# Entry into the attention stage: tile-wise pool waits, an earlier scale, an earlier table, a later first split

## The chip, the cores and the metric

The kernel runs as one program on one core of a Trainium2 chip. The metric is the device time of one execution in microseconds. Three executions of the kernel before took 1218.88, 1219.09 and 1220.08 us; the median, 1219.09 us, is the time before.

## What is computed

One layer of an encoder block on x of 1024 tokens by 1024 channels:

```python
u = rms_norm(x, g1)
q, k, v, cB, cC, cH, gA, gB = split(u @ w_in)        # 512 x 6, then 1024 x 2
q, k = rms_norm per head (8 heads of 64)
yA = neighbourhood_attention(q, k, v, rpb) @ w_attn_branch
yB = (cB * conv3(cC * cH)) @ w_conv_branch            # depthwise, width 3
x  = x + (sigmoid(gA) * yA + sigmoid(gB) * yB) @ w_o
x  = x + relu(rms_norm(x, g2) @ w_mlp_in)**2 @ w_mlp_out
```

The tokens form a grid of 16 rows by 64 columns. Each query sees a window of 8 rows by 16 columns, clamped inside the grid, with a learned bias.

## The kernel before

**Numbers.** Every operand of a product is held as two 16-bit floats, a high and a low part, and a product is three passes (high by high, high by low, low by high). A weight arrives as 32-bit "raw" pieces. Its chunk is scaled by a power of two and split: ScalarE writes the high part (L310), VectorE the low part (L301, `raw * scale - high`).

**How a chunk is prepared.** `Chunk.prep` is a Python generator that emits a few instructions at each resumption. For a conv chunk (kind C, four pieces of 128 x 768) it emits, in order:

1. four squares with a running sum on ScalarE (L263), one in each resumption;
2. the sum of the four and its product on VectorE (L267, L269), which writes one bf16 column of `ones`; then it waits until `units` has gone up by three;
3. the matmul by a matrix of ones that adds the column over the partitions (L201), on TensorE, into a bank of kind "d";
4. six resumptions on VectorE that turn the sum into a power of two and its products with the row gains (L204, L425, L427, L429, L431 with L432, L279);
5. the split, one piece in a resumption: ScalarE's high part of piece p beside VectorE's low part of piece p-1, and the load of a later raw piece on SyncE's queue.

`tick(n)` resumes the front generator of the list `bg` n times. While `forced[0]` is set, the waits on `units` inside the generators are passed over.

**The order around the change.** Everything is emitted in one program order for each engine, under a manual schedule; an engine takes its instructions strictly in that order. K's eight token blocks are finished by `qk_vec` (L612 to L632: ScalarE and VectorE in turn) and turned by a DMA transpose into `kD` (`finish_qk`, L643). After the last K products TensorE does two units of 24 matmuls for the first conv chunk into two banks of kind "o". Then the attention loop starts: 64 steps, and some more to empty the pipeline. Step k emits:

- the scores of step k into a bank of kind "s" (`at_qk`, L831), of which there are three, so step k waits until the maximum of step k-3 has been read;
- 7 or 8 conv matmuls (`emit`, L911);
- the bias and the maximum of step k-1 on VectorE (`at_max`, L845), which writes a tile `sz`;
- the exponential of step k-1 on ScalarE (`at_exp`, L854), the reciprocal of a pair of sums (L858, L859), the high part of the probabilities (L867, four steps behind) and the low part (L871, five behind);
- one step of the conv work (`conv_post`, `conv_taps`): ScalarE's copies of the two first banks into `z` (L719), the product with `z` (L724), the taps (L740, L744, and L747 and L750 on GpSimd);
- up to three resumptions of the background generator (`fill`), as long as `room()` holds. Two numbers in `debt` say how many ns of work VectorE and ScalarE have been given beyond 2150 ns a step, `spend` adds to them, and `room()` asks that both lie under 2350;
- from step 11 on, at odd steps, the product of the probabilities with V (`at_pv`, L888).

**Pools.** A pool may lie where closed pools lay. K's working tiles (`gq`, `qs`, `sq`, `q16`, `s16`) lie in `pqk`, closed just ahead of the attention loop; the loop's own tiles (`sz`, `z`, `cv`, `P16`, `PT`) lie in `p2`. In the kernel before, the pools `pbias`, `p2`, `wab`, `p3` and `p4` are opened without the argument `reuse_waits`, whose default is "pool": what first uses the new pool on an engine waits for everything that used the closed pools beneath it. With "tile", a tile waits for those old tiles alone whose bytes it takes over. In the layout of the program before, `z` lies over the last bytes of tiles of an earlier stage, over `gq` and over the start of one `s16`; the five `sz` lie over `s16`; the `q16` tiles, which the K transposes read, lie under `cv` alone. Pool `p5`, at the end, already has "tile".

**ScalarE's tables.** The exponential needs another activation table than the square root. The last square root of the K stage (L412) is in block 15 of `qk_vec`; the first exponential is that of attention step 0.

Of the kernel before, what the change touches and what calls it, by code (L numbers as in the profile page):

```python
# [14 lines left out]
AF = mybir.ActivationFunctionType  # L15
# [37 lines left out]
def encoder_block(ctx: ExitStack, tc: tile.TileContext, x, weights, cols, gqk, rel, masks, out):  # L53
    nc = tc.nc
    V, A, G, T, SP = nc.vector, nc.scalar, nc.gpsimd, nc.tensor, nc.sync
# [10 lines left out]
    def bank(tag):  # L66
        return psum.tile([128, 512], F32, name="ps_" + tag, tag=tag, bufs=banks[tag])
# [11 lines left out]
    sc = base.tile([128, 512], F32, name="sc")  # L79
# [3 lines left out]
    def cols_of(kind, n):  # L83
        a = area[kind]
        if a[1] + n > a[2]:
            assert kind != "keep"
            a[1] = a[0]
        a[1] += n
        return slice(a[1] - n, a[1])

    def keep(n=1):
        return cols_of("keep", n)

    def tmp(n=1):
        return cols_of("tmp", n)
# [25 lines left out]
    def advance(g):  # L121
        try:
            return next(g) or True
        except StopIteration:
            return False

    def step(n=1):
        for _ in range(n):
            for g in list(fg):
                if not advance(g):  # L130
                    fg.remove(g)

    def tick(n=1):

        for _ in range(n):
            i = 0
            while i < len(bg):
                r = advance(bg[i])
                if not r:
                    bg.pop(i)  # L140
                elif r == WAIT and side[0]:
                    i += 1
                else:
                    break
# [3 lines left out]
    def spend(v=0, a=0):  # L148

        debt[0] += v  # L150
        debt[1] += a

    def fill():

        i = 0
        while i < len(bg):
            r = advance(bg[i])
            if not r:
                bg.pop(i)
            elif r != WAIT:  # L160
                return True
            elif not side[0]:
                return False
            else:
                i += 1
        return False

    def drain():
        while fg:
            step()  # L170

    def flush():
        forced[0] = True
        while bg:
            tick()
            step()
        forced[0] = False

    late, units, forced, side = [], [0], [False], [False]
# [27 lines left out]
    def unit(mms, post=None, steps=0, ticks=0):  # L207

        for ps, l, r, a, b in mms:
            T.matmul(ps, l, r, start=a, stop=b)  # L210
        units[0] += 1
        work[0] += len(mms) * mms[0][0].shape[-1]
        settle()
        if post:
            late.append(post)
        for i in range(max(steps, ticks)):
            if i < steps:
                step()
            if i < ticks:
                tick()  # L220

    def settle():
        while late:
            late.pop(0)()


    wpool = {"ws": wsp}
# [109 lines left out]
    def push(*chunks):  # L337
        for ch in chunks:
            bg.append(ch.prep())
# [31 lines left out]
        SP.dma_start(xt[:, b], x[b * 128:(b + 1) * 128, :])  # L371

    gq = wqk.tile([128, 2, HD], F32, name="gq", bufs=1)
    warm = tmp()
    V.memset(sc[:, warm], 1.0)
    A.activation(sc[:, warm], sc[:, warm], AF.Sqrt)
    load_x(0)
# [231 lines left out]
    def qk_vec(ps, inv, kind, res):  # L609
        qs = wqk.tile([128, 512], F32, name="qs", bufs=3)  # L610
        sq = wqk.tile([128, 512], F32, name="sq", bufs=1)
        A.activation(qs, ps, AF.Copy, scale=sc[:, inv])  # L612
        A.activation(sq, qs, AF.Square)
        yield
        ss, y = tmp(8), tmp(8)
        V.tensor_reduce(sc[:, ss], sq.rearrange("p (h d) -> p h d", h=8), axis=AX, op=OP.add)
        yield
        yield from rstd(ss, HD, y, 12 if kind == "q" else 0)
        if kind == "k":
            V.tensor_scalar(sc[:, y], sc[:, y], sc[:, sgq], None, op0=OP.mult)  # L620
            yield
        q3 = qs.rearrange("p (h d) -> p h d", h=8)
        V.tensor_tensor(q3, q3, sc[:, y][:, :, None].to_broadcast([128, 8, HD]), op=OP.mult)
        yield
        if kind == "k":
            V.tensor_tensor(q3, q3, gq[:, 0][:, None, :].to_broadcast([128, 8, HD]), op=OP.mult)
        r = 2 if kind == "q" else 1
        t = wqk.tile([128, 8, 2, r, HD], F16, name=kind + "16", tag="q16")
        q4 = q3[:, :, None, :].to_broadcast([128, 8, r, HD])
        A.activation(t[:, :, 0], q4, AF.Copy)  # L630
        yield
        V.tensor_tensor(t[:, :, 1], q4, t[:, :, 0], op=OP.subtract)  # L632
        res.append(t)
# [4 lines left out]
    def finish_qk(n):  # L638
        kind, b = todo[n]
        while not q16[n]:  # L640
            step()
        dst = QD.rearrange("p a e w t -> p (a e w) t") if kind == "q" else KD
        SP.dma_start_transpose(dst[:, :, b * 128:(b + 1) * 128], q16.pop(n)[0].rearrange("p h w r d -> p (h w r d)"))  # L643

    for n, (kind, b) in enumerate(todo):
        ch = cQ if kind == "q" else cK
        if b == 0:
            push(cK if kind == "q" else cConv[0])
        ps = bank("do"[n % 2])
        q16[n] = []  # L650

        def post(ps=ps, kind=kind, n=n, ch=ch):
            fg.append(qk_vec(ps, ch.inv, kind, q16[n]))
        unit(tok_mms(ps, actU, b, ch, 8, 512, 0), post, 4, 6 if 4 < n < 8 else 3)
        if n == 3:
            forced[0] = True
            while formed[0] < 4:
                step()
            forced[0] = False
            QD = base.tile([128, 4, 2, 2, S], F16, name="qD", tag="Q")  # L660
            KD = base.tile([128, 8, S], F16, name="kD", tag="K")
            pln.close()
            base2 = ctx.enter_context(tc.tile_pool(name="base2", bufs=1))
            BT = base2.tile([128, 2, 4, S], F16, name="bT", tag="B")
            pbias = ExitStack()
            wbias = pbias.enter_context(tc.tile_pool(name="pbias", bufs=2))
            mk = wbias.tile([128, 2, 384], BF16, name="mk", bufs=1)
            SP.dma_start(mk, masks)
            cneg, cinv = keep(), keep()
            V.tensor_scalar(sc[:, cneg], sc[:, isgq], -(2.0 ** -15), None, op0=OP.mult)  # L670
            V.tensor_scalar(sc[:, cinv], sc[:, sgq], 2.0 ** 15, None, op0=OP.mult)
            bias = {0: bias_load(0)}
        if n >= 3:
            finish_qk(n - 3)
        if n in (5, 6):
            bias_make(*bias[0], n - 5)
        if b == 7:
            flush()
# [18 lines left out]
        step()  # L697
    settle()
    finish_qk(15)
    settle()  # L700
    drain()
    pqk.close()
    p2 = ExitStack()
    w2p = p2.enter_context(tc.tile_pool(name="p2", bufs=2))

    def perm(t, half=None):
        v = t.rearrange("p (r b c) -> p b r c", r=16, b=8)
# [97 lines left out]
    def room():  # L805
        return max(debt) < SPAN + 200
# [107 lines left out]
    for k in range(N + 16):  # L914
        p, w = k // 16, k % 16
        if p < 3 and w == 3:
            bias[p + 1] = bias_load(p + 1)
        if p < 3 and w in (12, 14):
            bias_make(*bias[p + 1], (w - 12) // 2)
            spend(550)  # L920
        ok = lambda d: 0 <= k - d < N
        debt[:] = [max(0, v - SPAN) for v in debt]
        spend(1200, 1120)
        if ok(0):
            at_qk(k)
        emit(4)
        if ok(1):
            at_max(k - 1)
        if ok(4):
            at_hi(k - 4)  # L930
        if k % 2 and ok(3):
            at_recip(k - 3)
        if ok(5):
            at_lo(k - 5)
        if k % 2 == 0 and ok(6):
            at_turn(k - 6)
        if ok(1):
            at_exp(k - 1)
        units[0] += 1
        conv_step(1)  # L940
        for _ in range(3):
            if not room() or not fill():
                break
        emit(3 if k < 14 or k % 4 == 0 else 4)
        if k % 2 == 1 and ok(11):
            at_pv(k - 11)
        if ok(14 + k % 2):
            at_out(k - 14 - k % 2, k % 2)
# [14 lines left out]


    p3 = ExitStack()
    wpool["wa"] = wpool["wb"] = p3.enter_context(tc.tile_pool(name="wab", bufs=2))
    w3p = p3.enter_context(tc.tile_pool(name="p3", bufs=2))
    M = (base.tile([128, 8, S], F16, name="mH", tag="K"), base.tile([128, 8, S], F16, name="mL", tag="V"))
    actA = lambda s, k: QD[:, k, 0, s]
    actB = lambda s, k: BT[:, s, k]  # L970
# [230 lines left out]

    p3.close()
    p4 = ExitStack()
    w4p = p4.enter_context(tc.tile_pool(name="p4", bufs=2))
    U2 = (u2T,
          w4p.tile([128, 3, 2, 4, 512], F16, name="u2x", bufs=1))
    HS = [dram.tile([128, 7, 4, 512], F32, name=f"hs{s}") for s in range(4)]
# [606 lines left out]
```

## Time and profile before

| | |
|---|---|
| median of three runs | 1219.09 us (1218.88 to 1220.08) |
| the profiled execution: its own time | 1219.86 us |
| its span, first to last instruction | 1218.0 us |
| TensorE busy | 1194.1 us, 98% |
| VectorE, ScalarE, GpSimd busy | 931.3, 764.4, 423.2 us |
| granted TensorE clock | 1.000 |
| chain that ended last, by engine | TensorE 74%, VectorE 15%, ScalarE 5%, DMA 3% |

The span is divided into the projections V, Q and K (to 147.6 us), the first two conv units (to 158.2), the attention loop beside the rest of the conv work (to 316.7), the gates and branches (to 548.6), the output projection with the second norm (to about 631), and the MLP. In a row of a timeline the first number is the start, the second the length; consecutive rows of one engine overlap by some 0.07 to 0.09 us. PE is TensorE, DVE VectorE, ACT ScalarE, POOL GpSimd; SPq and ACTq are the queues by which SyncE and ScalarE start DMAs. The bracket at the end of a row says how long the engine had been idle and what ended that.

### The profile page before, as it was taken

To read this page: it belongs to the slowest core of one execution; us is meant where nothing else is said; L and a number is where in the kernel's file an instruction comes from. 1 tells how busy PE (TensorE), PEld (TensorE's weight loads), DVE (VectorE), ACT (ScalarE), POOL (GpSimd) and SP (SyncE) were. 2 spreads that over 40 slices of the span, in tenths; PEclk is the share of its full clock that TensorE was granted. 3 is DMA by queue.
4 is the path that set the end of the run, shared out by engine and by line. 5 is a ranking of instruction groups with operands and counts; after the bars stand their busy time and mean duration, and the time that the engine had idled before them with its cause. 6 is when DMAs were issued, how large, how long until landed. Compare 5 with 4: busy or idle time off the path is not lost.

```text
span 1218.0 us, 17069 instructions
## 1 busy us (share of the span) xinstructions
PE 1194.1 (98%) x6294; PEld 572.9 (47%) x6294; DVE 931.3 (76%) x1758; ACT 764.4 (63%) x1186; POOL 423.2 (35%) x276
## 2 busy tenths in 40 slices
PE   5999999999999999999999999999999999999998
PEld 4544444454444444444458444444444444444444
DVE  6667878898468686887877665456448989998997
ACT  6786677777545455436668787687776754646440
POOL 1430003231411111101003465655657472553562
PEclk9999999999999999999999999999999999999999
DMA  7558555756651121226095654355375835335302
GB/s 279 106 186 182 113 124 114 154 111 118 133 143 54 51 69 35 70 62 246 19 184 131 208 190 160 129 187 166 129 284 199 314 127 203 143 134 195 104 35 104
DMA packets 170867, 173.35 MB, mean 142 GB/s; under 512 B 131488, under 2 KB 132000, under 8 KB 166688
## 3 DMA queue, kind: packets, MB, share of 16 engines
q1 hardware_dynamic: 170208, 168.07, 47.6%
q10 hardware_dynamic: 576, 4.19, 0.9%
q8 instruction: 49, 0.80, 0.3%
q14 instruction: 34, 0.28, 0.1%
HBM read 102.51 MB, written 37.75 MB: 115 GB/s over the span
## 4 chain that ended last, share of the span: by engine, by line
PE 74%; DVE 15%; ACT 5%; DMA 3%; issue 2%; SPq 0%; POOL 0%; ACTq 0%; DVEq 0%
PE ps_d L210 26%; PE ps_s L210 23%; PE ps_o L210 16%; PE ps_d L911 7%; DVE w_s L1033 2%; PE ps_s L831 1%; PE ps_o L888 1%; DVE w_ws L301 1%; DMA qD<-q 1%; DVE s L510 1%; DVE u L446 1%; DVE sg L1149 1%; DMA u2T<-v 1%; ACT w_ws L263 1%; DVE w_v L301 1%
## 5 line engine op out<-in xcount | busy, mean ns | idle before, releaser
L210 PEld LDWEIGHTS <-ops 128*128 128x128 f16 x1356 | 132.4, 98 | 157.3
L210 PEld LDWEIGHTS <-w 128*128 128x128 f16 x1368 | 132.8, 98 | 140.5 <-DMA u2T<-v 1.0
L911 PE MATMUL ps_d<-uT,w_ws 128*128 128x512 f16 x528 | 125.0, 379 | 0.0
L210 PE MATMUL ps_d<-ops 128*128 128x512 f16 (+1 forms) x528 | 118.3, 374 | 0.0
L1635 ACT ACTIVATE ops<-hf,sc 128x2048 f16<-128x2048 f32 x26 | 52.0, 2002 | 98.5 <-PE ps_o L210 35.9
L210 PE MATMUL ps_s<-ops 128*128 128x512 f16 x492 | 112.9, 379 | 0.0
L1022 POOL TENSOR_TENSOR tsum<-raw 128x512 f32<-128x512 f32 x28 | 45.8, 1648 | 148.9 <-ACT raw L1008 148.9
L210 PEld LDWEIGHTS <-uT 128*128 128x128 f16 x648 | 63.4, 99 | 68.2 <-issue 5.4
L1215 POOL TENSOR_TENSOR as<-as 128x512 f32<-128x512 f32 x56 | 77.5, 1385 | 40.8 <-ACT as L1495 37.5
L210 PEld LDWEIGHTS <-w_s 128*128 128x128 f16 x588 | 56.8, 98 | 69.5 <-DVE w_s L1033 2.0
L210 PE MATMUL ps_d<-u2x,w 128*128 128x512 f16 (+1 forms) x360 | 80.0, 372 | 0.0
L210 PE MATMUL ps_o<-ops 128*128 128x512 f16 x336 | 77.1, 379 | 0.0
L911 PEld LDWEIGHTS <-w_ws 128*128 128x128 f16 x528 | 51.0, 98 | 52.8
L1637 DVE SCALAR_TENSOR_TENSOR ops<-hf,sc,ops 128x2048 f16<-128x2048 f32 x26 | 72.6, 2791 | 3.5 <-ACT ops L1635 3.5
L1008 ACT ACTIVATE raw<-raw,sc 128x256 f32<-128x256 f32 x172 | 71.1, 496 | 1.9 <-DMA raw<-in_weights 1.9
L210 PE MATMUL ps_o<-u2T,w 128*128 128x512 f16 (+1 forms) x324 | 71.7, 371 | 0.0
L1022 POOL TENSOR_TENSOR gsum<-raw 128x512 f32<-128x512 f32 x14 | 19.0, 1377 | 133.8 <-issue 73.7
L1037 ACT ACTIVATE w<-raw,sc 128x512 f16<-128x512 f32 (+1 forms) x28 | 24.7, 929 | 52.3 <-DVE sc L431 52.3
L210 PE MATMUL ps_s<-u2T,w 128*128 128x512 f16 (+1 forms) x252 | 52.7, 359 | 0.0
L854 ACT ACTIVATE sz<-sz,sc 128x384 f32<-128x384 f32 (+1 forms) x64 | 37.4, 584 | 24.3 <-DVE sc L845 12.5
L1528 DVE TENSOR_TENSOR as<-ps_d,as 128x512 f32<-128x512 f32 (+1 forms) x14 | 9.4, 672 | 55.6 <-ACT as L1547 53.5
L310 ACT ACTIVATE w_ws<-raw,sc 128x512 f16<-128x512 f32 (+2 forms) x72 | 41.0, 638 | 15.6 <-DVE sc L279 15.6
(340 smaller groups left out, 2616.8 us busy)
## 6 DMA issues: line engine op xcount, KB each, us to landing
raw<-in_weights SPq DMA_DIRECT2D x89, 512.0 KB, 5.8
hs<-as SPq DMA_DIRECT2D x16, 1792.0 KB, 8.8
hf<-hs SPq DMA_DIRECT2D x26, 1024.0 KB, 6.7
w2x<-in_weights SPq DMA_DIRECT2D x16, 512.0 KB, 8.3
raw<-in_weights SPq DMA_DIRECT2D x16, 384.0 KB, 3.7
xt<-in_x SPq DMA_DIRECT2D x8, 512.0 KB, 10.1
gs<-s ACTq DMA_DIRECT2D x4, 1024.0 KB, 4.6
x<-in_x SPq DMA_DIRECT2D x8, 512.0 KB, 9.7
```

The source lines that it names most:

```text
L210: T.matmul(ps, l, r, start=a, stop=b)
L301: V.scalar_tensor_tensor(lo, self.raw[p][:, o:o + m], sc[:, c:c + 1], hi, op0=OP.mult, op1=OP.subtract)
L310: A.activation(self.parts[:, 0, f + o:f + o + m], self.raw[p][:, o:o + m], AF.Copy, scale=sc[:, c:c + 1])
L854: A.activation(z, z, AF.Exp, scale=-1.0, bias=sc[:, d["mx"]], accum_out=sc[:, d["sm"]])
L911: T.matmul(ps, l, r, start=a, stop=b)
L1008: A.activation(v, v, AF.Copy, scale=sc[:, at(g, 4 * i + k)])
L1022: G.tensor_tensor(t[:, o], a, b, op=OP.add)
L1033: V.scalar_tensor_tensor(o(1), w, sc[:, s], o(0), op0=OP.mult, op1=OP.subtract)
L1037: A.activation(o(0), w, AF.Copy, scale=sc[:, s])
L1215: sub.tensor_tensor(z[o], z[a], z[b], op=op)
L1635: A.activation(P[:, 1, 0], hf, AF.Copy, scale=sc[:, Rs])
L1637: V.scalar_tensor_tensor(P[:, 1, 1], hf, sc[:, Rs], P[:, 1, 0], op0=OP.mult, op1=OP.subtract)
```

## The change

Six things change, all in emission order or in waits; no arithmetic of the result does.

1. The pools `pbias`, `p2`, `wab`, `p3` and `p4` are opened with `reuse_waits="tile"`.
2. The scalar column `warm`, used at the start to load the square root's table, is kept, and after the last K block an exponential of this one column is emitted.
3. After that, ahead of the attention loop, the generator of the second conv chunk is resumed eight times with `forced` set: the matmul L201, the six VectorE resumptions L204 to L279, and ScalarE's high part of the first piece.
4. Steps 0 and 1 of the loop (the diff's k below 2) resume no background generator.
5. VectorE's fixed charge is 600 instead of 1200 ns in steps 0 to 4.
6. ScalarE's is 500 instead of 1120 ns in steps 0 to 3.

```diff
     gq = wqk.tile([128, 2, HD], F32, name="gq", bufs=1)
-    warm = tmp()
+    warm = keep()
     V.memset(sc[:, warm], 1.0)
     A.activation(sc[:, warm], sc[:, warm], AF.Sqrt)
...
-            wbias = pbias.enter_context(tc.tile_pool(name="pbias", bufs=2))
+            wbias = pbias.enter_context(tc.tile_pool(name="pbias", bufs=2, reuse_waits="tile"))
...
     settle()
     finish_qk(15)
+    A.activation(sc[:, warm], sc[:, warm], AF.Exp)
     settle()
     drain()
+    forced[0] = True
+    tick(8)
+    forced[0] = False
     pqk.close()
     p2 = ExitStack()
-    w2p = p2.enter_context(tc.tile_pool(name="p2", bufs=2))
+    w2p = p2.enter_context(tc.tile_pool(name="p2", bufs=2, reuse_waits="tile"))
...
-        spend(1200, 1120)
+        spend(1200 if k > 4 else 600, 1120 if k > 3 else 500)
...
         for _ in range(3):
-            if not room() or not fill():
+            if k < 2 or not room() or not fill():
                 break
...
-    wpool["wa"] = wpool["wb"] = p3.enter_context(tc.tile_pool(name="wab", bufs=2))
-    w3p = p3.enter_context(tc.tile_pool(name="p3", bufs=2))
+    wpool["wa"] = wpool["wb"] = p3.enter_context(tc.tile_pool(name="wab", bufs=2, reuse_waits="tile"))
+    w3p = p3.enter_context(tc.tile_pool(name="p3", bufs=2, reuse_waits="tile"))
...
-    w4p = p4.enter_context(tc.tile_pool(name="p4", bufs=2))
+    w4p = p4.enter_context(tc.tile_pool(name="p4", bufs=2, reuse_waits="tile"))
```

## Prediction, made before the result was known

> **What bounds the kernel now.** I read the page first, then TensorE's waits, then the timelines of all engines from 150 to 190 us, and last TensorE's few later waits.
>
> ```profile
> span 1218.0 us, 17069 instructions
> PE 1194.1 (98%) x6294; PEld 572.9 (47%) x6294; DVE 931.3 (76%) x1758; ACT 764.4 (63%) x1186; POOL 423.2 (35%) x276
> ...
> PE ps_o L201 <- DVE ones L332: 10.2, 1, 10.2
> ...
> PE ps_s L831 <- DVE sc L845: 2.4, 2, 1.6
> ```
>
> TensorE is the bound, and 24 us of the span are not its work. 10.2 of them are the start, which the change leaves alone. The largest wait after the start is that of the scores L831 for the maxima L845: twice, 2.4 us. The change can win such waits only. TensorE's timeline has them:
>
> ```profile
> 158.17 0.38 PE L831 MATMUL ps_s<-kD,qD 128*128 128x256 f16 x2
> ...
> 159.90 0.38 PE L831 MATMUL ps_s<-kD,qD 128*128 128x256 f16 x2
> ...
> 164.52 0.48 PE L831 MATMUL ps_s<-kD,qD 128*128 128x384 f16 x2 [0.86 <-DVE sc L845]
> ...
> 166.35 0.49 PE L831 MATMUL ps_s<-kD,qD 128*128 128x384 f16 x2
> ...
> 181.70 0.53 PE L888 MATMUL ps_o<-PT,vT 128*64 128x128 f16 x12
> 182.30 0.48 PE L831 MATMUL ps_s<-kD,qD 128*128 128x384 f16 x2
> ...
> 185.85 0.48 PE L831 MATMUL ps_s<-kD,qD 128*128 128x384 f16 x2 [1.55 <-DVE sc L845]
> ...
> 187.78 0.69 PE L888 MATMUL ps_o<-PT,vT 128*64 128x128 f16 x18
> 188.40 0.39 PE L831 MATMUL ps_s<-kD,qD 128*128 128x256 f16 x2
> ```
>
> These are the starts of steps 0, 1, 3, 4, 12, 13 and 14. Steps 0 to 13 take 188.40 - 158.17 = 30.23 us. Unhindered, a step with 256 columns takes 1.73 (159.90 - 158.17) and one with 384 takes 1.83 (166.35 - 164.52). The two products L888 add 0.46 (0.53, less the 0.07 by which the other one, 0.69 long, overlaps the row behind it) and 0.62, the scale's matmul 0.03. That is 2 x 1.73 + 12 x 1.83 + 1.11 = 26.53 us. So the entry loses 3.70 us: the two listed waits and smaller delays between them. After 188.40 the loop runs without one to 316 us. The 3.70 us are what this change is about, 0.30% of the time.
>
> Where they come from stands on the other engines:
>
> ```profile
> 158.56 0.16 DVE L269 TENSOR_TENSOR ones<-sc 128x1 bf16<-128x1 f32 x1
> ...
> 160.02 0.69 DVE L632 TENSOR_TENSOR k<-qs,k 128x512 f16<-128x512 f32 x1 [0.70 <-ACT k L630]
> 160.63 0.33 DVE L799 TENSOR_SCALAR sc<-sc 128x1 f32<-128x1 f32 x4
> 163.97 0.48 DVE L845 CUSTOM_DVE_ANT_0 sz<-ps_s,bias,sc 128x256 f32<-128x256 f32 x1 [3.02 <-DMA kD<-k]
> ...
> 164.78 0.61 DVE L845 CUSTOM_DVE_ANT_0 sz<-ps_s,biasm,sc 128x384 f32<-128x384 f32 x1
> ...
> 167.72 0.17 DVE L858 RECIPROCAL sc<-sc 128x2 f32<-128x2 f32 x1 [2.31 <-ACT sz L854]
> ...
> 167.99 0.68 DVE L724 TENSOR_TENSOR z<-ps_d,z 128x512 f32<-128x512 f32 x1
> 168.59 0.15 DVE L204 TENSOR_SCALAR sc<-ps_d 128x1 f32<-128x1 f32 x1
> ...
> 169.94 0.23 DVE L279 TENSOR_SCALAR sc<-sc 128x8 f32<-128x8 f32 x1
> ...
> 171.98 1.15 DVE L301 SCALAR_TENSOR_TENSOR w_ws<-raw,sc,w_ws 128x384 f16<-128x384 f32 x2 [0.62 <-ACT w_ws L310]
> ...
> 182.17 1.27 DVE L871 SCALAR_TENSOR_TENSOR P<-sz,sc,P 128x384 f16<-128x384 f32 x1
> 183.36 1.90 DVE L301 SCALAR_TENSOR_TENSOR w_ws<-raw,sc,w_ws 128x384 f16<-128x384 f32 x2
> 159.35 0.63 ACT L630 ACTIVATE k<-qs 128x512 f16<-128x512 f32 x1 [1.44 <-DVE qs L626]
> 163.90 1.37 ACT L719 ACTIVATE z<-ps_o,sc 128x512 f32<-128x512 f32 x2 [3.92 <-DMA kD<-k]
> 165.29 1.28 ACT L854 ACT_TABLE_LOAD   x1
> 166.59 0.51 ACT L854 ACTIVATE sz<-sz,sc 128x256 f32<-128x256 f32 x1
> 167.00 0.19 ACT L854 ACTIVATION_READ_ACCUMULATOR sz<-sz,sc 128x1 f32 x1
> 167.09 0.50 ACT L854 ACTIVATE sz<-sz,sc 128x256 f32<-128x256 f32 x1
> ...
> 171.34 2.12 ACT L310 ACTIVATE w_ws<-raw,sc 128x384 f16<-128x384 f32 x4
> 183.12 3.23 POOL L750 TENSOR_TENSOR cv<-cv,z 128x256 f32<-128x256 f32 x4
> ```
>
> VectorE's and ScalarE's first work in the loop waits for the last transposes of K, 3.02 and 3.92 us, though the scores of step 0 need only the first blocks of `kD` and run at 158.17. Then the exponential waits for its table, VectorE for the exponential (2.31). VectorE is then late; while GpSimd is in L750 its own operations take twice their time (1.90 instead of 1.15), and the maximum of step 10 is 1.55 us late for TensorE.
>
> **The change part by part.** I carry the clocks forward in the new order; durations are those rows, less the overlap of 0.08.
>
> *The earlier scale.* L201 now stands ahead of step 0 in TensorE's queue, which is in order. Its `ones` column is ready at 158.56 + 0.16 = 158.72, TensorE at 158.17. It waits, and step 0 begins at 158.78: cost 0.61 us. That is the one new wait; behind it stands all of the attention stage. The six VectorE resumptions move into the hole behind L632. From L204's start to the end of L279's issue took 1.5 us with a maximum between them; without it about 1.1: 160.63 to 161.7.
>
> *Tile-wise waits in `p2`.* By the layout `z` and `sz` lie over tiles whose readers are VectorE's of block 15 (over by 160) and stores of long ago, so the K transposes hold nothing. With the four L799 (0.28) the first maximum starts at 162.0 instead of 163.97.
>
> *Table.* ScalarE is free at 159.98; load and one element take 1.28 + 0.2, to 161.4, in a hole that ended at 163.90. Cover gone, it costs 1.3. The Trainium skill ("ScalarE: Activation LUTs", What ACT_TABLE_LOAD costs) gives a drain of about 1.38 us behind the load, 2.66 in all. Here the exponential starts 0.02 us after the load, so I take 1.28. By the page's figure, an estimate, ScalarE would run 1.4 us later and the gain would be 1.6 instead of 2.6 us.
>
> *The new order of the splits.* Debt by hand: step 2 starts at 600 and 500, so two resumptions fit (1028 for each low part, 912 for each high part); step 3 fits one, step 4 the last. Four pieces, before in steps 5 to 10, are done in steps 2 to 4. ScalarE: the high part of piece 0 from 161.85 (after L279) to 162.87, `z` twice to 164.26, two exponentials of 0.50 to 165.26, piece 1 with its first half ready at 165.8. VectorE: two maxima of 0.41 to 162.82, low part 0 (1.06) to 163.9, *idle to 165.85 for piece 1*, low part 1 to 166.9, maximum 2 to 167.45. Step 5 needs that at 158.78 + 2 x 1.73 + 3 x 1.83 = 167.73: just in time. Then reciprocal (0.28), L724 (0.60), low part 2 (1.06), maximum 3 ready at 170.02. Step 6 is due at 169.58: a wait of 0.44. Maximum 4 is ready at 171.6, step 7 due at 171.85. No splits follow, and VectorE's lead grows. The slowing beside L750 (0.66 and 0.75 us in the rows) meets a lead of about 2.3 us at step 13.
>
> *At nothing.* The memsets, the kept column, `pbias` (its first DMA is issued at 68.0):
>
> ```profile
> L668 SPq DMA_DIRECT2D mk<-in_masks x1: 392/392/392, 68.0 to 68.0; - x1
> ...
> 322.90 1.71 ACT L310 ACTIVATE w_wa<-raw,sc 128x256 f16<-128x256 f32 x4 [2.67 <-POOL bT L774]
> ...
> 316.25 0.53 PE L888 MATMUL ps_o<-PT,vT 128*64 128x128 f16 x12 [0.19 <-DMA PT<-P]
> ...
> 351.24 2.33 PE L210 MATMUL ps_d<-qD,w_s 128*128 128x512 f16 x10 [0.21 <-DVE w_s L1033]
> 650.84 1.48 PE L210 MATMUL ps_d<-u2T,w 128*128 128x256 f16 x12 [0.74 <-DMA u2T<-v]
> ```
>
> In `wab` the first split stops waiting for GpSimd's end of the last conv chunk, 2.67 us, but TensorE runs on other chunks there. Its three waits from 316 us on come from a DMA of probabilities, from a split that follows TensorE's own scale matmul, and from the last norm's DMA, none of them a pool's. SyncE's queue now takes the raw loads of the next chunk three to six steps earlier, ahead of the bias load and the first transpose of `P`; the last of them waits for low part 3 (171.0), and that transpose is ready only at 173. It stays covered.
>
> Sum: 3.70 lost before; 0.61 + 0.44 and rounding, 1.1, lost after: 2.6 us gained. The profiled execution (span 1218.0, own time 1219.86) would become 1215.4 and 1217.3. The median is 0.77 below that execution: 1219.09 - 2.6 = 1216.5 us.
>
> Bounds: the idle of VectorE for piece 1 can be up to 0.5 longer or shorter with ScalarE's order, which makes the waits of steps 5 and 6 between 0 and 1.0; the gain lies between 2.0 and 3.1.
>
> **Rivals.**
>
> 1. *The old wait stays*, for some tile of K under `sz` or `z`. The maxima start at 163.97 again and ScalarE's `z` at 163.90; pieces 1 and 2 follow 1.0 us later. Then step 3 waits 0.33, step 5 0.49, step 6 0.64, with L201's 0.61 some 2.1 us: gain 1.6, 1217.5 us. For it: the argument decides by layout, not by a row. Against: in that layout only `cv` touches `q16`.
> 2. *Slower: L201 is held with the rest.* If its operand or bank is tied to what now waits for `kD` (landing 163.90), TensorE stands from 158.17: 5.7 us, less the 3.70, and 0.4 for step 6: 2.4 us slower, 1221.5. It decides from a hold of 3.3 us on, that is from 161.5. For it: before, L201 ran at step 2 and any hold up to there was unseen. Against: the row of L269 at 158.56.
> 3. *Later waits go too*: all three rows above, 1.14 us, as the pools `p3` and `p4` wait less: 3.7 gained, 1215.4. Against: their releasers.
>
> **How the numbers follow.** A measurement of this kernel tells about 0.2% (2.44 us) from no change, so the forecast lies at the border: of its band from 2.0 to 3.1, six tenths and a little more lie beyond 2.44. Forecast 0.68 (0.44 faster, 0.24 same); rival 1 0.11 (same), rival 2 0.08 (slower), rival 3 0.13 (faster). Faster 0.57, same 0.35, slower 0.08. The range takes in the forecast's band (1216.0 to 1217.1), rivals 1 and 3, and the scatter of the medians shown (up to 1.0): 1215.0 to 1218.6; it leaves out rival 2.
>
> **What would show it.** TensorE: a wait of some 0.6 at L201 near 158.2, none at step 3, one of 0 to 1 us at step 5 or 6, none at step 13; step 14 near 185.8. VectorE: first L845 near 162.0, an L301 that waits 2 us for L310 in step 2. ScalarE: the table load near 160.0. It is wrong if the first L845 still waits for `kD`, if L201 waits more than 1 us, or if a wait appears behind 316 us.

## The result and the profile after

The changed kernel took 1217.09 us (median of 12 executions, 1215.36 to 1218.75), the kernel before 1219.99 us on the same chips: a ratio of 0.9975, 95% interval 0.9967 to 0.9983, or 2.9 us less. The forecast was 2.6 us less, from 1219.09 to 1216.5 us; the median of the kernel before is now 0.9 us higher than the one it started from. The spans of the two profiled executions differ by 2.6 us, 1218.0 against 1215.4.

In the changed kernel a line behind the early exponential has a number larger by four: L831, L845, L854 are L835, L849, L858. In the versions below that leave out lines of the change the shift is smaller, three in a_notable and one in v_both. First TensorE, waits (in total, times, longest) and timeline:

```profile
PE ps_o L201 <- DVE ones L332: 10.2, 1, 10.2
...
PE ps_d L210 <- DMA u2T<-v: 0.3, 1, 0.3
...
PE ps_d L201 <- DVE ones L269: 0.2, 1, 0.2
148.84 10.52 PE L210 MATMUL ps_o<-uT,w_ws 128*128 128x512 f16 x48
159.52 0.16 PE L201 MATMUL ps_d<-ones 128*128 128x1 bf16 x1 [0.16 <-DVE ones L269]
159.62 0.38 PE L835 MATMUL ps_s<-kD,qD 128*128 128x256 f16 x2
...
168.58 0.49 PE L835 MATMUL ps_s<-kD,qD 128*128 128x384 f16 x2
...
170.65 0.48 PE L835 MATMUL ps_s<-kD,qD 128*128 128x384 f16 x2
...
186.61 0.39 PE L835 MATMUL ps_s<-kD,qD 128*128 128x256 f16 x2
```

The waits for the maxima, 2.4 us in two, are gone from the list. L201 waits a little; between steps 5 and 6 (168.58, 170.65) 0.24 us are lost. I measure every kernel by its *entry*: from the moment at which TensorE is ready for what follows the two conv units (the end of their row, less the 0.17 by which such a row overlaps the next) to the scores of step 14. It was 30.23 us before (158.17 to 188.40) and is 27.42 now (159.19 to 186.61): 2.81 less. The expectations of the first four runs count it from the end of the row, which makes it 27.25.

This execution reached the entry 1.02 us later than that of before. Most of that, 0.87, is there by the last wait of the V projection (31.68 against 30.81), where both kernels do the same work. Behind the entry it gained 0.8 us in smaller waits, of which a second execution of the kernel before gains about 0.5 as well. So neither can be put down to the change, and that the two spans differ by just the predicted 2.6 is in part luck.

VectorE and ScalarE:

```profile
161.37 0.15 DVE L204 TENSOR_SCALAR sc<-ps_d 128x1 f32<-128x1 f32 x1
...
162.70 0.48 DVE L849 CUSTOM_DVE_ANT_0 sz<-ps_s,bias,sc 128x256 f32<-128x256 f32 x1
...
166.45 1.15 DVE L301 SCALAR_TENSOR_TENSOR w_ws<-raw,sc,w_ws 128x384 f16<-128x384 f32 x2 [1.80 <-ACT w_ws L310]
160.75 1.28 ACT L700 ACT_TABLE_LOAD   x1
162.04 0.20 ACT L700 ACTIVATE sc<-sc 128x1 f32<-128x1 f32 x1
162.58 1.12 ACT L310 ACTIVATE w_ws<-raw,sc 128x384 f16<-128x384 f32 x2 [0.34 <-DVE sc L279]
163.60 1.35 ACT L723 ACTIVATE z<-ps_o,sc 128x512 f32<-128x512 f32 x2
```

The first maximum no longer waits for `kD`; ScalarE goes from K's last block through the table, the first split and `z` without a wait for it; and VectorE stands 1.80 us in step 2 for the high part of piece 1, as worked out (2.0).

### The profile page after: what moved, and what is told of

Its sections match the earlier page's. It is cut to its first block, busy times and chain, and to the rows that moved or that the text cites. A ratio compares the mean times of both kernels' runs of the same rounds, so it can differ in the third digit from the quotient of the medians.

```text
span 1215.4 us, 17071 instructions
## 1 busy us (share of the span) xinstructions
PE 1194.7 (98%) x6294; PEld 574.1 (47%) x6294; DVE 936.7 (77%) x1758; ACT 764.2 (63%) x1187; POOL 424.3 (35%) x276
## 4 chain that ended last, share of the span: by engine, by line
PE 86%; DVE 9%; ACT 2%; DMA 1%; issue 1%; SPq 0%; POOL 0%; DVEq 0%; ACTq 0%
PE ps_d L210 31%; PE ps_s L210 24%; PE ps_o L210 19%; PE ps_d L915 9%; PE ps_s L835 2%; DVE w_s L1037 2%; PE ps_o L892 2%; DVE sg L1153 1%; DMA u2T<-v 1%; DMA raw<-in_weights 1%; DVE w_ws L301 0%; ACT w_s L1041 0%; DVE sc L321 0%; DVE m L1155 0%; ACT sg L1119 0%
## 5 line engine op out<-in xcount | busy, mean ns | idle before, releaser
L858 ACT ACTIVATE sz<-sz,sc 128x384 f32<-128x384 f32 (+1 forms) x64 | 37.2, 581 | 24.6 <-DVE sc L849 14.2
```

The source lines that it names most:

```text
L858: A.activation(z, z, AF.Exp, scale=-1.0, bias=sc[:, d["mx"]], accum_out=sc[:, d["sm"]])
```

## The experiments

Theory A is the prediction's: the waits of `p2` for K's transposes are the main thing removed. Theory B: the gain is the scale and the splits, taken out of the steps where VectorE is late. Theory C: the later pools give part of it. Names with a_ start from the changed kernel, with b_ from the one before, v_ is a version of the changed one.

| kernel | ready | step 14 | entry, us | ratio to before, 95% interval |
|---|---|---|---|---|
| before | 158.17 | 188.40 | 30.23 | |
| changed | 159.19 | 186.61 | 27.42 | 0.9975 (0.9967 to 0.9983) |
| a_pool | 159.24 | 188.02 | 28.78 | 0.998 (0.997 to 0.999) |
| a_noscale | 158.20 | 185.12 | 26.92 | 0.9962 (0.9947 to 0.9977) |
| b_p2 | 158.26 | 185.17 | 26.91 | 0.9967 (0.9954 to 0.998) |
| b_late | 159.04 | 189.28 | 30.24 | 0.9993 (0.9983 to 1.0002) |
| b_all | 158.07 | 184.98 | 26.91 | 0.9972 (0.9961 to 0.9984) |
| a_notable | 158.44 | 187.58 | 29.14 | 0.9985 (0.9976 to 0.9994) |
| a_order | 158.51 | 186.73 | 28.22 | 0.9981 (0.9972 to 0.999) |
| v_both | 158.92 | 185.72 | 26.80 | 0.9964 (0.995 to 0.9978) |
| before_again | 158.21 | 188.45 | 30.24 | one execution, 1219.35 us |
| a_nolate | 158.97 | 186.68 | 27.71 | one execution, 1217.65 us |
| b_p2_again | 157.83 | 184.75 | 26.92 | one execution, 1216.38 us |

The entry of the kernel before and of b_p2 comes back within 0.01 us in a second execution, while the ratios have intervals of 0.1% and more, that is 1 us and more. So differences of some tenths are read from the entry. Where L201 stands ahead of step 0 one thing disturbs it: TensorE loses 0.33 us there in the changed kernel's profile, but 0.61 to 0.62 in a_pool, a_notable, a_order and a_nolate. That is why a_nolate, whose entry has the same code as the changed kernel's, takes 27.71 instead of 27.42. So I give differences from the changed kernel against both profiles.

**a_pool: the changed kernel, `p2` waits as a pool**

```diff
-    w2p = p2.enter_context(tc.tile_pool(name="p2", bufs=2, reuse_waits="tile"))
+    w2p = p2.enter_context(tc.tile_pool(name="p2", bufs=2))
```

> The changed kernel, but p2 waits as a pool again; all else stays changed. 'Entry' is the time from the end of the two first conv units on TensorE to the scores of step 14: 30.23 us before, 27.25 in the changed kernel (159.36 to 186.61). Theory A (the waits for K's transposes are the main thing removed): the first maximum waits for kD again, near 164; ScalarE's z too; waits return at steps 3, 5 and 6; entry about 28.6, so 1.0 to 1.4 us slower than the changed kernel and 1.5 faster than before, ratio to before about 0.9987. Theory B (the gain is the scale and the splits taken out of the steps, the pool wait was covered): entry about 27.3, ratio as for the changed kernel, 0.9975. Theory C (the later pools give part of it): entry 28.6, but the waits at the last norm's DMA (0.74 before, 0.34 after) stay short.

```profile
165.06 0.48 DVE L849 CUSTOM_DVE_ANT_0 sz<-ps_s,bias,sc 128x256 f32<-128x256 f32 x1 [1.94 <-DMA kD<-k]
165.00 1.37 ACT L723 ACTIVATE z<-ps_o,sc 128x512 f32<-128x512 f32 x2 [0.95 <-DMA kD<-k]
165.61 0.48 PE L835 MATMUL ps_s<-kD,qD 128*128 128x384 f16 x2 [0.19 <-DVE sc L849]
...
169.59 0.48 PE L835 MATMUL ps_s<-kD,qD 128*128 128x384 f16 x2 [0.15 <-DVE sc L849]
172.06 0.48 PE L835 MATMUL ps_s<-kD,qD 128*128 128x384 f16 x2 [0.47 <-DVE sc L849]
```

The maximum and `z` wait for `kD` again, and the scores wait at steps 3, 5 and 6, the three of theory A. Entry 28.78, 1.36 longer than changed and 1.07 longer than a_nolate. Theory B falls as an account of the whole, but 1.45 us of the gain (30.23 - 28.78) are there without the edit to `p2`. Theory C is not touched: the wait for the last norm's DMA is 0.34 here.

**a_noscale: the changed kernel without the forced resumptions**

```diff
-    forced[0] = True
-    tick(8)
-    forced[0] = False
```

> The changed kernel without the eight forced resumptions: the scale of the second conv chunk is made in steps 2 to 4 again and its four pieces are split from step 5 on. Theory A: TensorE does not wait ahead of step 0, the first maximum is near 161.5, nothing holds steps 5 and 6, a wait of 0 to 0.4 comes at step 13 beside GpSimd's work; entry 26.6 to 27.0, that is 0.3 to 0.6 us shorter than the changed kernel; the early scale costs rather than brings. Theory B: the late splits make VectorE late again, entry 28 to 30, 1 to 3 us slower than the changed kernel.

Entry 26.92. Nothing holds TensorE before step 0 or at steps 5 and 6. The early scale costs 0.50 us against the changed kernel and 0.79 against a_nolate.

**b_p2: the kernel before, with `p2` tile-wise and nothing else**

```diff
-    w2p = p2.enter_context(tc.tile_pool(name="p2", bufs=2))
+    w2p = p2.enter_context(tc.tile_pool(name="p2", bufs=2, reuse_waits="tile"))
```

> The kernel before with one edit: p2 waits tile by tile. Table, scale and splits as before. Theory A: the first maximum moves from 163.97 to about 161, VectorE has 3 us more, the table load falls into that lead; entry 26.6 to 27.0, ratio to before 0.997: this edit alone gives the whole gain and more. Theory B: VectorE still waits 2.3 us for the exponential behind the table load and meets GpSimd's work late; entry 29 to 30, ratio 0.999 or above.

Entry 26.91: one argument gives 3.32 us, more than the whole change's 2.81. Its VectorE, ScalarE and later VectorE rows show why the rest isn't needed:

```profile
160.97 0.47 DVE L845 CUSTOM_DVE_ANT_0 sz<-ps_s,bias,sc 128x256 f32<-128x256 f32 x1
...
162.35 0.62 DVE L845 CUSTOM_DVE_ANT_0 sz<-ps_s,biasm,sc 128x384 f32<-128x384 f32 x1 [0.50 <-PE ps_s L831]
...
163.78 0.17 DVE L858 RECIPROCAL sc<-sc 128x2 f32<-128x2 f32 x1 [0.80 <-ACT sz L854]
...
178.94 1.27 DVE L871 SCALAR_TENSOR_TENSOR P<-sz,sc,P 128x384 f16<-128x384 f32 x1
180.13 1.90 DVE L301 SCALAR_TENSOR_TENSOR w_ws<-raw,sc,w_ws 128x384 f16<-128x384 f32 x2
159.99 1.35 ACT L719 ACTIVATE z<-ps_o,sc 128x512 f32<-128x512 f32 x2
161.35 1.28 ACT L854 ACT_TABLE_LOAD   x1
```

The first maximum is at 160.97 instead of 163.97. With the third, VectorE has caught up with TensorE and waits for it (0.50), so the table load and the 0.80 behind it cost nothing. And the slowing beside GpSimd's L750 is all there, 1.27 and 1.90 as before; it just meets a VectorE that is 3 us ahead, and no wait follows.

**b_late: the kernel before, with the four other pools (`pbias`, `wab`, `p3`, `p4`, all alike) tile-wise**

```diff
-            wbias = pbias.enter_context(tc.tile_pool(name="pbias", bufs=2))
+            wbias = pbias.enter_context(tc.tile_pool(name="pbias", bufs=2, reuse_waits="tile"))
...
```

> The kernel before with the tile-wise waits of pbias, wab, p3 and p4 alone. Theory A: nothing on TensorE's path, entry 30.2, the three waits behind 316 us (0.19, 0.21, 0.74) within 0.1 us, ratio 1.000 within 0.0005. Theory C: the wait of 0.74 falls to about 0.34 and that of 0.19 goes, 0.6 us faster, ratio 0.9995.

Entry 30.24, the two waits of before (0.87 and 1.55) in place. The wait for the last norm's DMA is 0.25, that for the probabilities is gone, which speaks for theory C; the ratio's interval holds both 1.000 and 0.9995. Three more executions below bear on this.

**b_all: the kernel before, with the edits of b_p2 and b_late and no other**

> The kernel before with the tile-wise waits of all five pools and nothing else. Theory A (the p2 wait is the whole of the gain in the entry): entry 26.9 as in the run with p2 alone (26.91), step 14 near 185.2, ratio 0.9965 or a little below; so the four other edits bring nothing. Theory D (the wait of 0.48 for a transpose into uT that the run with p2 alone showed behind 316 us comes from the pools of the gates still waiting): that wait is gone here, the s4T transposes start 1 to 2 us earlier. If it is there again, its cause is the DMA queue's own timing.

Entry 26.91; no wait for a transpose into `uT`, which b_p2 has behind the entry (0.48, see below). So the other edits (table, charges, gate, early scale) bring nothing once the pools wait by tile: b_all and a_noscale differ by 0.01.

**a_notable: the changed kernel without the early exponential**

```diff
-    A.activation(sc[:, warm], sc[:, warm], AF.Exp)
```

> The changed kernel without the early exponential: the table load of 1.28 us stands ahead of the first exponential again. By the clocks of the prediction, piece 1's high part comes 1.3 us later, VectorE waits 3.3 us for it in step 2, and the scores wait about 1.1 at step 5 and 0.6 at step 6; entry about 28.7 instead of 27.42, ratio about 0.9985. Rival: the load hides in VectorE's idle time behind it as well, entry unchanged within 0.2.

```profile
169.16 0.48 PE L834 MATMUL ps_s<-kD,qD 128*128 128x384 f16 x2 [0.88 <-DVE sc L848]
171.62 0.49 PE L834 MATMUL ps_s<-kD,qD 128*128 128x384 f16 x2 [0.47 <-DVE sc L848]
```

Entry 29.14, 1.72 longer than changed; 0.28 of that is L201's larger loss, and against a_nolate it is 1.43. The waits are at steps 5 and 6 as said. In the changed kernel the early table is needed, because the splits of step 2 put ScalarE's high part 1, and with it VectorE, behind it.

**a_order: the changed kernel with the old charges and no gate at step 2**

```diff
-        spend(1200 if k > 4 else 600, 1120 if k > 3 else 500)
+        spend(1200, 1120)
...
-            if k < 2 or not room() or not fill():
+            if not room() or not fill():
```

> The changed kernel with the old charges (1200, 1120) and splits allowed from step 0: low part 0 and high part 1 are emitted in step 0, ahead of the first maximum, the rest in steps 1 to 3. By the clocks the first maximum moves to about 163.5 relative to a start of 158.17, the scores wait 0.5 at step 4 and 0.4 at step 6; entry about 28.0 instead of 27.42, 0.5 us slower than the changed kernel. Rival (the charges and the gate at k = 2 do nothing, since VectorE has room): entry 27.4.

Entry 28.22, 0.80 longer than changed and 0.51 longer than a_nolate, with waits at steps 4 and 6 (0.16 and 0.26 listed). VectorE's low part of piece 0 now starts at 162.83, ahead of the first maximum at 163.90. Gate and charges serve the early scale: without it, old (b_all) or new (a_noscale) ones give the same entry. What each of the two does alone was not run.

**v_both: the scale behind the first conv matmuls, one resumption a step**

```diff
         emit(4)
+        if k == 0:
+            forced[0] = True
+            tick(8)
+            forced[0] = False
...
-        for _ in range(3):
+        for _ in range(1 if k < 6 else 3):
```

(The forced resumptions ahead of the loop are taken out.)

> The changed kernel, with the eight forced resumptions moved behind the first four conv matmuls of step 0, and one resumption a step instead of up to three in steps 2 to 5. By the clocks TensorE waits neither at L201 (its column is ready before) nor at steps 5 and 6; entry 26.5 to 26.9, 0.5 to 0.9 us shorter than the changed kernel (27.42) and no longer than that without the early scale (26.92); ratio 0.9965. Rival: the splits collide with the taps at steps 7 to 9 and a wait appears there.

Entry 26.80: with both of the changed kernel's own waits taken away it is 0.62 shorter than changed, 0.91 shorter than a_nolate, and 0.11 shorter than b_p2. No wait for a maximum appears later either. This one, a_noscale, b_p2 and b_all beat the kernel before, and by the entry they are 0.5 to 0.6 us ahead of the changed one; the intervals of their ratios overlap with its own and can't show that.

Its steps 11 to 14 show what the end of the entry takes where nothing waits:

```profile
178.93 0.49 PE L832 MATMUL ps_s<-kD,qD 128*128 128x384 f16 x2
...
181.32 0.50 PE L832 MATMUL ps_s<-kD,qD 128*128 128x384 f16 x2
...
183.17 0.49 PE L832 MATMUL ps_s<-kD,qD 128*128 128x384 f16 x2
...
185.72 0.39 PE L832 MATMUL ps_s<-kD,qD 128*128 128x256 f16 x2
```

The steps with the product with V take 2.39 and 2.55 us, 0.56 and 0.72 more than the plain 1.83, where the prediction added 0.46 and 0.62.

**Three more executions: before_again, a_nolate, b_p2_again**

The first and the last repeat a kernel. a_nolate is the changed kernel with b_late's edit taken back:

```diff
-    w4p = p4.enter_context(tc.tile_pool(name="p4", bufs=2, reuse_waits="tile"))
+    w4p = p4.enter_context(tc.tile_pool(name="p4", bufs=2))
...
```

> The kernel before, unchanged, looked at once more, for the scatter of a single profile. If the wait for the last norm's DMA (0.74 in the first profile) and the moment at which TensorE is ready for step 0 (158.17) are scatter, they move here by some tenths and up to 1 us; the entry should not: 30.2 within 0.1.

> The changed kernel with p2 tile-wise, but pbias, wab, p3 and p4 as pools again. If the later pools matter, a wait for a transpose into uT near 356 us appears as in the run with p2 alone (0.48), and the wait for the last norm's DMA is near 0.8; if both are the DMA queue's own scatter, they lie anywhere between 0 and 0.9. Entry 27.4.

> The kernel before with p2 tile-wise alone, looked at once more. If the wait of 0.48 for a transpose into uT comes from the gates' pools, it is here again; if it is scatter of the DMA queue it is gone or of another size. Entry 26.9 within 0.1.

The kernel before, unchanged, shows 0.36 us for the last norm's DMA where it had shown 0.74, and no wait for the probabilities. In its two profiles, from the chain of waits, the row that starts that DMA's chain and the DMA itself; then the same two of the changed kernel and of b_p2:

```profile
631.78 0.76 DVE x L1398
...
641.92 8.87 DMA u2T<-v
631.69 0.76 DVE x L1398
...
641.83 8.49 DMA u2T<-v
629.55 0.76 DVE x L1402
...
639.69 8.48 DMA u2T<-v
628.49 0.76 DVE x L1398
...
638.62 9.03 DMA u2T<-v
```

Ahead of the DMA the chain takes 10.13 or 10.14 us in all four, whatever the pools do; the wait follows the landing, 8.48 to 9.03. With all five pools tile-wise a_noscale waits 0.83, and with the later ones as pools b_p2_again waits 0.24. That part of theory C falls.

Another wait remains. In three executions `p2` waits by tile and the later pools as pools, and each waits for a transpose into `uT`; here b_p2, a_nolate and b_p2_again, and behind them the same products in v_both, which has all five tile-wise, and in the changed kernel:

```profile
355.85 2.55 PE L210 MATMUL ps_d<-uT,w_s 128*128 128x512 f16 x11 [0.48 <-DMA uT<-gs]
357.17 2.55 PE L210 MATMUL ps_d<-uT,w_s 128*128 128x512 f16 x11 [0.30 <-DMA uT<-gs]
356.14 2.55 PE L210 MATMUL ps_d<-uT,w_s 128*128 128x512 f16 x11 [0.99 <-DMA uT<-gs]
355.54 3.00 PE L210 MATMUL ps_d<-uT,w_s 128*128 128x512 f16 x12
356.42 2.75 PE L210 MATMUL ps_d<-uT,w_s 128*128 128x512 f16 x12
```

v_both lists no wait, but its twelve products take 3.00 us where the five others with all five pools tile-wise (changed, a_noscale, b_all, a_notable, a_order) take 2.75. What divides these nine is SyncE: ahead of the transposes into `uT` and `s4T` its queue issues sixteen others, here in v_both and in the changed kernel:

```profile
309.34 23.33 SPq L985 DMA_TRANSPOSE qD<-gs  x16
310.29 21.68 SPq L984 DMA_TRANSPOSE qD<-gs  x16
```

The sixteen take 23.16 to 23.33 us in the four with a delay and 21.61 to 22.62 in the five without. In b_p2 and b_p2_again one of the eight issues into `uT` also takes 1.76 and 2.20 us, where the median is 1.26. Before, before_again and b_late, where TensorE is not ahead, and a_pool, half as far ahead, show no delay. So an earlier TensorE can meet the transposes of the gates, at 0.25 to 1.0 us, when SyncE issues slowly. All three executions with the later pools as pools are among the slow ones, but so is v_both. Whether those pools slow SyncE or this is its scatter is not shown, and with it the rest of theory C.

## Why the prediction was right, and where it was not

- *What bounds the entry.* Right: VectorE's and ScalarE's first work waited for K's transposes without need, a_pool and b_p2 show it from both sides.
- *The sum.* 27.62 us were forecast for the entry (158.17 to 185.79, the 3.70 us of waits less 2.6), measured 27.42, and 27.71 in a_nolate, which has the same entry code. That it comes so near is partly luck, as two errors cancel. Without any such wait the entry takes 26.80 (v_both), not 26.53, mainly because the products with V cost more; so 3.43 us were to be had of the 3.70. Lost after the change were 0.62 us, 0.91 in a_nolate, instead of 1.1.
- *L201's wait.* 0.61 forecast. In the changed kernel's profile 0.33 (159.19 to 159.52), because TensorE came 1.02 us later in that execution and VectorE only 0.74; in a_pool, a_notable, a_order and a_nolate 0.61 to 0.62.
- *Step 6.* 0.44 forecast, 0.24 measured (0.23 in a_nolate); nothing at step 5. The term was too large by 0.2.
- *The first maximum.* Forecast 3.83 us after TensorE is ready, measured 3.51, and 3.79 in a_nolate, where L201's loss is as forecast; the chain L204 to the four scalings took 1.33 (161.37 to 162.70), against 1.4.
- *The table.* Forecast at 1.28 and covered. The Trainium skill ("ScalarE: Activation LUTs", What ACT_TABLE_LOAD costs) adds a drain of 1.38; here the next operation starts at 162.04, 0.01 behind the end of the load, so the measurement decides for 1.28. Nor does a drain stand ahead of the load, which follows `z` in the kernel before within 0.02 us (163.90 + 1.37, 165.29). The price without cover, forecast at 1.3, was 1.43 in a_notable, against a_nolate with the same loss at L201.
- *Rival 1* (the old wait stays) gave 1.6 us of gain; a_pool, where it does stay, has 1.45 (30.23 - 28.78). *Rival 2* did not occur: L201 depends on its column alone. *Rival 3* did not occur: of the three later waits, the 0.19 is missing from the kernel before itself in before_again, the 0.21 stands in every kernel, and the 0.74 follows the DMA's landing.
- *At nothing.* For the later pools neither refuted nor shown to be right. "TensorE runs on other chunks there" held for the rows of before; with TensorE 3 us ahead the transposes into `uT` can come late, with either setting of these pools. The prediction asked what else comes late only inside the entry.
- *Not asked.* The prediction costed the change as a whole and took every edit as part of the path. b_p2 shows that 3.32 us hang on one of them, a_noscale that the early scale takes 0.5 to 0.8 back, and b_all that table, charges and gate bring nothing without it; they only repair what the early scale moves. The prediction did not carry its clocks forward for the old order with the first maximum at 161; b_p2 has that order, its first maximum at 160.97, and no score that waits for a maximum.

## What to carry to other kernels

When a pool is opened over closed ones, look at what its first users wait for: a wait for a whole pool can hang on the last DMA of the stage before, though that DMA reads no byte that they take over. Price each edit of a bundle alone and in company: here the other edits together were worth 1.45 us while the wait stayed (a_pool) and less than nothing once it was gone, since a lead of 3 us hid the table load, the late splits and GpSimd's slowing at once. And an operation brought forward in an in-order queue waits where it now stands: L201 cost 0.6 us ahead of step 0 and nothing four matmuls behind its start.

## What was not expected of the hardware

Two executions of b_p2 reach the entry at 158.26 and 157.83 us, and over all kernels, whose code ahead of it does the same work, it is reached between 157.83 and 159.24: a scatter of 1.4 us, half of what was to be measured. In the profiles of the changed kernel and of v_both the granted TensorE clock was 0.91 from 20 to 40 us, and 1.00 there in all others and in every entry; so the entries can be compared. The same transpose, of the same tile behind the same chain, landed in 9.03 us in one execution of b_p2 and in 8.38 in the other.
